# Keeping silu(g) and the rotary's swapped product in PSUM, and moving the first expert weights' splits ahead of the convolution's layer norm

## The chip, the cores and the metric

The kernel runs on one core of one Trainium2 chip. The metric is the device time of one execution in microseconds, as the median of several runs. The engines are TensorE (PE, with its weight loads as PEld), VectorE (DVE), ScalarE (ACT), GpSimd (POOL) and SyncE (SP), which here only issues DMA transfers.

## What is computed

Two layers over 256 tokens of width 1024. Each has a mixer and a feed-forward part, each followed by a residual layer norm. The mixer projects the input to six parts: a gated pair for a causal depthwise convolution of 31 taps, q and k (rotated), v, and a gate g. In the first layer the feed-forward part is a dense SwiGLU, in the second a mixture of 8 experts, two for each token. Everything is float32. Cut to what matters:

```python
glu_a, glu_b, q, k, v, g = split(x @ w_in)
u = silu(layer_norm(causal_conv(glu_a * sigmoid(glu_b)) + conv_b))
r = retention(rotary(q), rotary(k) / 8, v)          # 4 heads, chunks of 64
r = silu(g) * (group_norm(r) * ret_gn_g)
mix = concat([u, r]) @ w_out
x = layer_norm(ALPHA * x + mix)
# rotary: x1 * cos - x2 * sin, x1 * sin + x2 * cos
# layer 0: f = swiglu(x); layer 1: f = the two chosen experts' swiglu, weighted by their gates
x = layer_norm(ALPHA * x + f)
```

## The kernel before

**Split products.** A float32 product is made of three fast ones (`mm3`, lines 152 to 156): each operand is split into a high part and a rest, and high x high, high x rest and rest x high are summed. A split (`parts`, lines 107 to 110) is a cast on ScalarE (L109) and a subtraction on VectorE, or on GpSimd where `eng` is `gp` (both are L110). Weights come in units of 1 MB, 128 x 2048; each is loaded by one DMA into a buffer (`fetch`, L132) and split as two halves. `plan` fixes the order of all units and the engine of each half (lines 165 to 197); `W.take()` hands out the next half and `W.ahead(n)` splits up to n halves in advance. The order of instructions on each engine is the order of the program text, since the schedule is manual. All weight loads are issued by SyncE in that order, as soon as a buffer is free. Buffers are taken from a list (`seq`): seven `raw` buffers in the mixers; behind them the list is set anew to one `raw`, six `raw2` and four `raw`, then two of `once` and the one of `main`, and then repeats 13 buffers.

**Mixer** (`mixer`, lines 367 to 639). VectorE does the convolution one tap at a time (L387, L391), reading the input `u` from SBUF and its running sum from PSUM; `fill(n)` puts n of these steps between other work, and `fill(-1)` does the rest. The last 11 or 12 taps of the fourth channel block go to TensorE (`taps`, L407). Rotary (lines 437 to 446), per token tile: the swapped halves times sine into `t2` (L441, twice), the product with cosine into `qk` (L444), and their sum (L446). Then retention, its group norm (`gnorm`: statistics on VectorE, L489 on ScalarE, a multiply by `gn` on GpSimd, L492), the projection of g, the taps, and per token tile silu(g) into `sgt` (L584) and its product with `rz` (L585). TensorE transposes `rz` (L497), ScalarE copies it to `mr` (L498), and the retention half of the output product runs for three of four accumulators (L506). When the convolution is done, its transposes (L516), its layer norm (`conv_ln`, with the power L250 on GpSimd) and the convolution half of the output product follow. All PSUM tiles of this phase come from one pool of eight banks (`bank`).

**From mixer 1 to the experts.** The layer norm of token tile 0 is shared out over VectorE, ScalarE and GpSimd, that of tile 1 is on VectorE (L259 to L278). Then x is transposed (L291), copied (L292), multiplied with the router (`logits`, L320), and `choose` picks two experts per token (lines 303 to 316, tiny VectorE operations). x is split into high and rest as well (`parts`, tile 0 with GpSimd). Behind this the ranks `rk` are formed (L724 to L731), the selection `P` (L742), and `gather` collects the tokens of two experts by products with `P` (L751), whose results are split again (`gah`, `gal`, `gbh`, `gbl`). The experts' loop takes 56 blocks of six units each.

**What the change and the prediction touch.** `plan` for the experts (line 192); `rotary` (439); `sgt` (577, 584, 585); the places of `W.ahead(2)` and `W.ahead(4)` (628, 638); `parts` of x tile 0 (627) against `choose(0)` (629).

Of the kernel before, what the change touches and what calls it, by code (L numbers as in the profile page):

```python
# [11 lines left out]
F32 = mybir.dt.float32  # L12
# [3 lines left out]
AF = mybir.ActivationFunctionType  # L16
ALU = mybir.AluOpType
# [9 lines left out]
NT = S // 128  # L27
# [17 lines left out]
MOEP = {1: 0}  # L45
# [29 lines left out]
def tile_hybrid(ctx: ExitStack, tc, xT_in, x_in, ws, wm, cols, lnp, gnp, router, ident_in, rot, mask_in, out):  # L75
    nc = tc.nc
    v, sc, pe, gp = nc.vector, nc.scalar, nc.tensor, nc.gpsimd
# [13 lines left out]
    def f32(ap):  # L91
        return ap.bitcast(F32)
# [5 lines left out]
    def tok(t):  # L98
        return slice(128 * t, 128 * t + 128)

    def half(h):
        return slice(512 * h, 512 * h + 512)
# [4 lines left out]
    def parts(hi, lo, src, eng=None):  # L107

        sc.copy(hi, src)  # L109
        (eng or v).tensor_tensor(lo, src, f32(hi), op=ALU.subtract)  # L110
# [35 lines left out]
    W = Stream(emit)  # L146

    def plan(src, eng=None, kinds=("first", "second")):
        unit = src if isinstance(src, Unit) else Unit(src, eng)
        W.items += [(k, unit) for k in kinds]  # L150
# [14 lines left out]
    for l in range(DEPTH):  # L165
        b = l * MIXU
# [21 lines left out]
    for i, (e, b) in enumerate(blocks):  # L188
        prev_w2 = [wm[blocks[i - 1][0], 6 * blocks[i - 1][1] + q] for q in (4, 5)] if i else []
        for q in range(4):  # L190
            first = i == 0 and q < 2
            plan(Unit(wm[e, 6 * b + q], tuple(gp if first and q == 0 or MOEP.get(q) == h else None for h in range(2)),
                      at=0 if first and q else None))
        for w in prev_w2:
            plan(w)
# [21 lines left out]
    x = main.tile([128, NT, D], F32, tag="x", name="x")  # L217
# [68 lines left out]
    def turn_x(t, psum):  # L286

        for k in range(0, KD, 4):
            p = psum.tile([128, 4, 128], F32, tag="wk", name="wk")
            for j in range(4):  # L290
                pe.transpose(p[:, j, :], x[:, t, 128 * (k + j):128 * (k + j) + 128], ident)  # L291
            sc.copy(xf[:, k:k + 4, tok(t)], p)  # L292

    def part_x():
        for k in range(0, KD, 4):
            parts(xh[:, k:k + 4, :], xl[:, k:k + 4, :], xf[:, k:k + 4, :])

    xn = [w.rearrange("p (t k) s -> p t (k s)", t=NT) for w in X]
# [4 lines left out]
    def choose(t, lg):  # L303

        for n, (m, s) in enumerate(((m1, s1), (m2, s2))):
            v.tensor_reduce(m[:, t:t + 1], lg, axis=AX.X, op=ALU.max)
            q = sm.tile([128, NE], F32, tag="rq", name="rq")
            v.scalar_tensor_tensor(q, lg, m[:, t:t + 1], ie[:, t, :], op0=ALU.is_equal, op1=ALU.mult)
            i = sm.tile([128, 1], F32, tag="ri", name="ri")
            v.tensor_reduce(i, q, axis=AX.X, op=ALU.min)  # L310
            v.tensor_scalar(s[:, t, :], ie[:, t, :], i[:, 0:1], None, op0=ALU.is_equal)
            if n == 0:
                l2 = sm.tile([128, NE], F32, tag="rl", name="rl")
                v.scalar_tensor_tensor(l2, s1[:, t, :], -3.0e38, lg, op0=ALU.mult, op1=ALU.add)
                lg = l2
        v.tensor_tensor(sel[:, t, :], s1[:, t, :], s2[:, t, :], op=ALU.add)

    def logits(pl, t):
        for k in range(KD):
            pe.matmul(pl[:, t, :], xf[:, k, tok(t)], rt[:, k, :], start=k == 0, stop=k == KD - 1, skip_group_check=True)  # L320
# [8 lines left out]
    def bank(psum, shape):  # L329
        return psum.tile(shape, F32, tag="wk", name="wk")  # L330
# [36 lines left out]
    def mixer(l, psum, mp, me, heads, then):  # L367
# [8 lines left out]
        qkT = mp.tile([128, 2, 2, S], F32, tag="qkT", name="qkT")  # L376
        qk = mp.tile([128, NT, 512], F32, tag="qk", name="qk")
        PT = mp.tile([128, H, 384], F32, tag="PT", name="PT")
        rz = me.tile([128, NT, 512], F32, name="rz")
# [29 lines left out]
        def fill(n):  # L409

            while convs and n:
                g = convs.pop(0)
                if next(g, 0) is None:
                    convs.insert(1, g)
                    n -= 1
# [11 lines left out]
        def proj():  # L427

            ps = [bank(psum, [128, 512]) for t in range(NT)]
            for k in range(0, KD, 2):  # L430
                w = view(W.take(), "p (k f) -> p k f", k=2)
                for t, p in enumerate(ps):
                    for j in range(2):
                        mm3(p, two(X, A, k + j, tok(t)), two(w, A, j), k + j == 0, k + j == KD - 1)
            return ps

        def rotary(t, p):
            pv = p.rearrange("p (g s d) -> p g s d", g=8, s=2)
            t2 = me.tile([128, 8, 2, 32], F32, tag="t2", name="t2")
            for s in range(2):  # L440
                v.tensor_tensor(t2[:, :, s, :], pv[:, :, 1 - s, :],  # L441
                                rott[:, t, 1, 32 * s:32 * s + 32].unsqueeze(1).to_broadcast([128, 8, 32]), op=ALU.mult)
            o = qk[:, t, :].rearrange("p (g d) -> p g d", g=8)
            v.tensor_tensor(o, p.rearrange("p (g d) -> p g d", g=8),  # L444
                            rott[:, t, 0, :].unsqueeze(1).to_broadcast([128, 8, 64]), op=ALU.mult)
            v.tensor_tensor(qk[:, t, :], qk[:, t, :], t2.rearrange("p g s d -> p (g s d)"), op=ALU.add)  # L446
# [19 lines left out]
        def retain(t):  # L466
            p = bank(psum, [128, H, DV])
            for h in range(H):
                for j in range(t + 1):
                    c0 = 256 if j else 128 * t  # L470
                    pe.matmul(p[:, h, :], PT[:, h, c0:c0 + 128], vt[:, j, 128 * h:128 * h + 128],
                              start=(j == 0), stop=(j == t), skip_group_check=True)
            return p
# [20 lines left out]
        def turn_r(t):  # L494
            p = bank(psum, [128, 4, 128])
            for k in range(4):
                pe.transpose(p[:, k, :], rz[:, t, 128 * k:128 * k + 128], ident)  # L497
            sc.copy(mr[:, :, tok(t)], p)  # L498
# [4 lines left out]
        def wout_r(t, h):  # L503
            acc[t][h] = bank(psum, [128, 512])
            for k in range(4):
                pe.matmul(acc[t][h], mr[:, k, tok(t)], Wr[k // 2][:, k % 2, half(h)], start=k == 0, stop=False,  # L506
                          skip_group_check=True)
# [66 lines left out]
        fill(next(F))  # L574
        glu(3)
        fill(next(F))
        sgt = mp.tile([128, NT, 512], F32, tag="qkT", name="sgt")
        pr = [retain(t) for t in range(NT)]
        gnorm(pr)
        pg = proj()  # L580
        taps()
        fill(next(F))
        for t in range(NT):
            sc.activation(sgt[:, t, :], pg[t], AF.Silu)  # L584
            v.tensor_tensor(rz[:, t, :], rz[:, t, :], sgt[:, t, :], op=ALU.mult)  # L585
            fill(next(F))
        if l == 0:
            nc.sync.dma_start(x, x_in)
# [3 lines left out]
        for t in range(NT):  # L592
            turn_r(t)
        Wc += [W.take(0) for _ in range(4)]
        wout_r(0, 0)
        wout_r(0, 1)
        wout_r(1, 0)
# [26 lines left out]
                    heads = then(psum)  # L624
            ln_end(t, x, s, st, gt, ASIDE and l > 0 and t == 0)
        if l > 0:
            parts(xn[0][:, 0, :], xn[1][:, 0, :], x[:, 0, :], gp)
            W.ahead(2)
            choose(0, pl[:, 0, :])
        turn_x(NT - 1, psum)  # L630
        if l == 0:
            part_x()
            W.ahead(3)
        else:
            logits(pl, 1)
            parts(xn[0][:, 1, :], xn[1][:, 1, :], x[:, 1, :])
            choose(1, pl[:, 1, :])
            W.ahead(4)
        return heads


# [51 lines left out]
    with tc.tile_pool(name="ps1", bufs=8, space=bass.MemoryType.PSUM) as psum:  # L693
        busy(WARM, bank(psum, [128, 512]))
        with (tc.tile_pool(name="mp0", bufs=1, side="right", reuse_waits="tile") as mp,
              tc.tile_pool(name="me0", bufs=1, side="right", reuse_waits="tile") as me):
            heads = mixer(0, psum, mp, me, [], head)
        with tc.tile_pool(name="dp", bufs=1, side="right", reuse_waits="tile") as dp:
            heads = dense(psum, dp, heads)
        with (tc.tile_pool(name="mp1", bufs=1, side="right", reuse_waits="tile") as mp,  # L700
              tc.tile_pool(name="me1", bufs=1, side="right", reuse_waits="tile") as me):
            mixer(1, psum, mp, me, heads, None)
# [113 lines left out]
    def tokens_of(e0):  # L816
        pls = ((mo, "ga"), (mo, "gb") if e0 % 4 == 0 else (late[0], "gc"))
        g = gather(lambda i, t: rk[:, t, e0 + i:e0 + i + 1], 2, pls, mo if e0 % 4 == 0 else late[0])
        gs, PT = next(g)
        for i in range(2):  # L820
            got[e0 + i] = (gs[i], PT[:, i, :])
        return g
# [3 lines left out]
            pass  # L826

    g0 = tokens_of(0)
    cnt = mo.tile([128, 1], F32, name="cnt")
    v.tensor_reduce(cnt, pr[:, 2, :], axis=AX.X, op=ALU.max)  # L830
    cnti = mo.tile([128, 1], I32, name="cnti")
# [261 lines left out]
```

## Time and profile before

| | |
|---|---|
| median of 3 runs | 1488.01 us (1486.11 to 1498.08) |
| the profiled run | 1490.48 us, its span 1488.7 us |
| PE busy | 1438.5 us, 97% of the span |
| DVE busy | 1234.3 us, 83% |
| ACT busy | 973.8 us, 65% |
| POOL busy | 276.1 us, 19% |
| loads from HBM | 433.69 MB, 292 GB/s over the span |

Layer 0's mixer takes the first 120 us, the dense part the time to about 350, layer 1's mixer to about 454; the experts begin at 473.6 with the gather and run to about 1480. The table's shares are means over these stages, which have different limits. A timeline row has start, duration, engine, line, operation, output and inputs, shapes and the number of instructions that it merges; in brackets stands the engine's idle time before it and what ended that. A `q` behind an engine means its sequencer or queue.

### The profile page before, as it was taken

What the parts mean: (1) busy time and instruction counts of PE and PEld (TensorE: products, weight loads), DVE (VectorE), ACT (ScalarE), POOL (GpSimd) and SP (SyncE); (2) the same over time, 40 slices, a digit from 0 to 9 for tenths busy, and PEclk for the clock granted to TensorE, in tenths of its full rate; (3) what the DMA queues carried; (4) which work ended last, traced back from release to release, by engine and by line L of the source; (5) the groups of instructions that cost most, each with busy time, mean ns of one, the idle gap of its engine ahead of it and who ended that gap; (6) DMA issues with size and microseconds to landing.
All of it is one profiled execution on the core that took longest, in us unless ns stands there. A gap on an engine that the chain in (4) does not pass through costs nothing. (4 is left out here: it accounts for less than half of the span.)

```text
span 1488.7 us, 19729 instructions
## 1 busy us (share of the span) xinstructions
PE 1438.5 (97%) x7385; PEld 1208.2 (81%) x7385; DVE 1234.3 (83%) x1401; ACT 973.8 (65%) x1153; POOL 276.1 (19%) x138
## 2 busy tenths in 40 slices
PE   9989999999987999999999999999999999999995
PEld 8859999998856887778878877888887888888884
DVE  7976455547987899889899998999899899999896
ACT  6334344434443877768877767777877777787773
POOL 5630000002844113111111111111111111111111
PEclk9999999999997999999999999999999999999998
DMA  9535544545547888979999997999998899999951
GB/s 368 208 113 227 194 175 183 211 161 182 183 164 310 311 312 336 343 300 356 382 342 378 367 356 302 368 371 352 378 376 304 342 376 354 363 373 370 353 216 59
DMA packets 62311, 436.10 MB, mean 293 GB/s; under 512 B 7040, under 2 KB 7424, under 8 KB 9856
## 3 DMA queue, kind: packets, MB, share of 16 engines
q1 hardware_dynamic: 61920, 434.24, 77.4%
q8 instruction: 60, 0.98, 0.3%
q10 hardware_dynamic: 288, 0.52, 0.1%
q14 instruction: 43, 0.35, 0.1%
HBM read 433.69 MB, written 1.05 MB: 292 GB/s over the span
## 5 line engine op out<-in xcount | busy, mean ns | idle before, releaser
L110 DVE TENSOR_TENSOR wl<-raw,wh 128x1024 fp32r<-128x1024 f32 (+1 forms) x704 | 880.5, 1289 | 61.2 <-ACT wh L109 35.8
L109 ACT CAST wh<-raw 128x1024 fp32r<-128x1024 f32 (+1 forms) x802 | 820.8, 1045 | 160.2 <-PE ac L156 94.7
L110 POOL TENSOR_TENSOR wl<-raw,wh 128x1024 fp32r<-128x1024 f32 x98 | 241.9, 2484 | 1107.3 <-ACT wh L109 1062.5
L155 PE MATMUL ac<-wl,gah 128*128 128x512 f32 x448 | 175.2, 391 | 2.8 <-DVE wl L110 2.3
L154 PE MATMUL ac<-wh,gah 128*128 128x512 f32 x448 | 177.4, 396 | 0.0
L154 PE MATMUL y<-wh,hth 128*128 128x512 f32 x440 | 172.8, 393 | 3.6 <-DVE ys1l L110 3.6
L155 PE MATMUL y<-wl,hth 128*128 128x512 f32 x440 | 172.0, 391 | 3.8 <-DVE wl L110 3.8
L156 PE MATMUL ac<-wh,gal 128*128 128x512 f32 x448 | 175.1, 391 | 0.0
L156 PE MATMUL y<-wh,htl 128*128 128x512 f32 x448 | 174.5, 390 | 0.0
L154 PE MATMUL wk<-xh,wh 128*128 128x256 f32 x512 | 145.4, 284 | 1.8 <-ACT wh L109 1.8
L156 PE MATMUL wk<-xh,wl 128*128 128x256 f32 x512 | 145.0, 283 | 0.2 <-DVE wl L110 0.2
L155 PE MATMUL wk<-xl,wh 128*128 128x256 f32 x512 | 144.7, 283 | 0.0
L391 DVE SCALAR_TENSOR_TENSOR wk<-u,colt,wk 128x256 f32<-128x256 f32 x209 | 99.8, 489 | 5.7
L154 PEld LDWEIGHTS y<-wh,hth 128*128 128x128 f32 x440 | 82.6, 188 | 24.3 <-DVE ys1l L110 6.6
L155 PEld LDWEIGHTS ac<-wl,gah 128*128 128x128 f32 x448 | 84.4, 188 | 21.4 <-DVE wl L110 3.6
L155 PEld LDWEIGHTS y<-wl,hth 128*128 128x128 f32 x440 | 82.6, 188 | 22.4 <-DVE wl L110 5.6
L154 PEld LDWEIGHTS wk<-xh,wh 128*128 128x128 f32 x512 | 97.4, 190 | 3.4 <-ACT wh L109 2.2
L156 PEld LDWEIGHTS wk<-xh,wl 128*128 128x128 f32 x512 | 99.1, 194 | 0.7 <-DVE wl L110 0.7
L156 PEld LDWEIGHTS ac<-wh,gal 128*128 128x128 f32 x448 | 84.3, 188 | 17.8
L156 PEld LDWEIGHTS y<-wh,htl 128*128 128x128 f32 x448 | 84.1, 188 | 17.4
L155 PEld LDWEIGHTS wk<-xl,wh 128*128 128x128 f32 x512 | 97.5, 190 | 0.9
L154 PEld LDWEIGHTS ac<-wh,gah 128*128 128x128 f32 x448 | 84.4, 188 | 16.6
(202 smaller groups left out, 2055.1 us busy)
## 6 DMA issues: line engine op xcount, KB each, us to landing
raw<-in_wm_dram SPq DMA_DIRECT2D x336, 1024.0 KB, 7.0
raw<-in_ws_dram SPq DMA_DIRECT2D x68, 1024.0 KB, 5.0
raw<-in_lnp_dram SPq DMA_DIRECT2D x4, 1024.0 KB, 5.0
raw<-in_ws_dram SPq DMA_DIRECT2D x8, 256.0 KB, 5.5
xf<-in_xT_dram SPq DMA_DIRECT2D x4, 256.0 KB, 4.7
x<-in_x_dram SPq DMA_DIRECT2D x1, 1024.0 KB, 7.5
mask<-in_mask_dram SPq DMA_DIRECT2D x1, 768.0 KB, 12.7
gn<-in_gnp_dram SPq DMA_DIRECT2D x2, 256.0 KB, 8.3
```

The lines of the kernel that those rows point to most:

```text
L109: sc.copy(hi, src)
L110: (eng or v).tensor_tensor(lo, src, f32(hi), op=ALU.subtract)
L154: pe.matmul(o, a[0], b[0], start=first, stop=False, skip_group_check=True)
L155: pe.matmul(o, a[0], b[1], start=False, stop=False, skip_group_check=True)
L156: pe.matmul(o, a[1], b[0], start=False, stop=last, skip_group_check=True)
L391: v.scalar_tensor_tensor(d, u[:, cc, k:k + S], w[:, k:k + 1], o, op0=ALU.mult, op1=ALU.add)
```

## The change

- The rotary's swapped product `t2` becomes a PSUM tile from the pool of eight banks instead of an SBUF tile. L441 writes it and L446 reads it as before.
- silu(g) is written in place over `pg` in PSUM; the SBUF tile `sgt` goes, and the product with `rz` reads `pg`.
- The first two halves of the experts' weights (first unit, both with GpSimd as before) are split ahead of the first output products of mixer 1, instead of behind its last layer norm.
- x tile 0 is split with VectorE instead of GpSimd, behind `choose(0)` instead of ahead of it.
- The second unit's first half is split with VectorE instead of GpSimd, and both of its halves come behind the selection `P` of the first gather (`tokens_of(0)`), when the list of buffers has been set anew, instead of ahead of it.

```diff
@@ -189,7 +189,7 @@
         prev_w2 = [wm[blocks[i - 1][0], 6 * blocks[i - 1][1] + q] for q in (4, 5)] if i else []
         for q in range(4):
             first = i == 0 and q < 2
-            plan(Unit(wm[e, 6 * b + q], tuple(gp if first and q == 0 or MOEP.get(q) == h else None for h in range(2)),
+            plan(Unit(wm[e, 6 * b + q], tuple(gp if (q == 0 if first else MOEP.get(q) == h) else None for h in range(2)),
                       at=0 if first and q else None))
         for w in prev_w2:
             plan(w)
@@ -436,7 +436,7 @@
 
         def rotary(t, p):
             pv = p.rearrange("p (g s d) -> p g s d", g=8, s=2)
-            t2 = me.tile([128, 8, 2, 32], F32, tag="t2", name="t2")
+            t2 = bank(psum, [128, 8, 2, 32])
             for s in range(2):
                 v.tensor_tensor(t2[:, :, s, :], pv[:, :, 1 - s, :],
                                 rott[:, t, 1, 32 * s:32 * s + 32].unsqueeze(1).to_broadcast([128, 8, 32]), op=ALU.mult)
@@ -574,15 +574,14 @@
         fill(next(F))
         glu(3)
         fill(next(F))
-        sgt = mp.tile([128, NT, 512], F32, tag="qkT", name="sgt")
         pr = [retain(t) for t in range(NT)]
         gnorm(pr)
         pg = proj()
         taps()
         fill(next(F))
         for t in range(NT):
-            sc.activation(sgt[:, t, :], pg[t], AF.Silu)
-            v.tensor_tensor(rz[:, t, :], rz[:, t, :], sgt[:, t, :], op=ALU.mult)
+            sc.activation(pg[t], pg[t], AF.Silu)
+            v.tensor_tensor(rz[:, t, :], rz[:, t, :], pg[t], op=ALU.mult)
             fill(next(F))
         if l == 0:
             nc.sync.dma_start(x, x_in)
@@ -592,6 +591,8 @@
         for t in range(NT):
             turn_r(t)
         Wc += [W.take(0) for _ in range(4)]
+        if l > 0:
+            W.ahead(2)
         wout_r(0, 0)
         wout_r(0, 1)
         wout_r(1, 0)
@@ -624,9 +625,8 @@
                     heads = then(psum)
             ln_end(t, x, s, st, gt, ASIDE and l > 0 and t == 0)
         if l > 0:
-            parts(xn[0][:, 0, :], xn[1][:, 0, :], x[:, 0, :], gp)
-            W.ahead(2)
             choose(0, pl[:, 0, :])
+            parts(xn[0][:, 0, :], xn[1][:, 0, :], x[:, 0, :])
         turn_x(NT - 1, psum)
         if l == 0:
             part_x()
@@ -635,7 +635,6 @@
             logits(pl, 1)
             parts(xn[0][:, 1, :], xn[1][:, 1, :], x[:, 1, :])
             choose(1, pl[:, 1, :])
-            W.ahead(4)
         return heads
 
 
@@ -826,6 +825,7 @@
             pass
 
     g0 = tokens_of(0)
+    W.ahead(4)
     cnt = mo.tile([128, 1], F32, name="cnt")
     v.tensor_reduce(cnt, pr[:, 2, :], axis=AX.X, op=ALU.max)
     cnti = mo.tile([128, 1], I32, name="cnti")
```

## Rows read from the trace of the kernel before

**Rows 1.** The page's first line: the span.

```profile
span 1488.7 us, 19729 instructions
```

**Rows 2.** Busy us by stretch: PE, PEld, DVE, ACT, POOL, clock, DMA, GB/s.

```profile
15.00:76.10 61.10, 61.10 (x371) 53.86 (x370) 55.67 (x125) 31.54 (x53) 44.98 (x20) 1.00 0.71 279
...
76.10:80.80 4.70, 1.58 (x10) 1.35 (x10) 4.46 (x5) 1.14 (x3) 4.70 (x3) 0.83 0.13 16
...
421.76:426.40 4.64, 1.15 (x9) 0.91 (x9) 4.61 (x5) 0.59 (x1) 3.54 (x2) 1.00 0.58 201
...
454.00:473.60 19.60, 12.12 (x84) 10.70 (x83) 16.73 (x35) 7.91 (x10) 13.38 (x8) 0.60 0.83 319
...
600.00:1450.00 850.00, 840.06 (x3815) 689.45 (x3816) 773.95 (x703) 655.90 (x714) 118.11 (x48) 1.00 0.92 349
```

**Rows 3.** Timeline of PE, both mixers and the router.

```profile
43.26 0.39 PE L156 MATMUL wk<-wh,xl 128*128 128x512 f32 x1
...
43.49 1.04 PE L452 MATMUL wk<-ident,qk 128*128 128x128 f32 x8
...
77.12 0.65 PE L497 MATMUL wk<-ident,rz 128*128 128x128 f32 x4 [1.02 <-DVE rz L585]
...
79.87 1.11 PE L497 MATMUL wk<-ident,rz 128*128 128x128 f32 x4 [2.10 <-DVE rz L585]
...
80.78 11.37 PE L506 MATMUL wk<-raw,mr 128*128 128x512 f32 x24
...
426.40 10.47 PE L506 MATMUL wk<-raw,mr 128*128 128x512 f32 x24
...
465.94 3.55 PE L320 MATMUL wk<-rt,xf 128*128 128x8 f32 x16 [1.40 <-DVE rl L314]
```

**Rows 4.** VectorE by source line: calls, ns min/median/max, first and last start.

```profile
L446 DVE TENSOR_TENSOR qk<-qk,t x4: 691/1993/2848, 37.8 to 383.7; 128x512 f32<-128x512 f32 x4
...
L585 DVE TENSOR_TENSOR rz<-rz,sgt x4: 801/2629/2825, 76.3 to 423.4; 128x512 f32<-128x512 f32 x4
...
L444 DVE TENSOR_TENSOR qk<-wk,rott x4: 676/680/682, 37.1 to 383.0; 128x512 f32<-128x512 f32 x4
```

**Rows 5.** Timeline of ACT, both mixers.

```profile
75.53 1.13 ACT L584 ACTIVATE sgt<-wk 128x512 f32<-128x512 f32 x2
...
396.11 0.39 ACT L420 ACTIVATE sgl<-wk 128x256 f32<-128x256 f32 x1 [4.96 <-PE wk L156]
```

**Rows 6.** Timeline of DVE, rotary and end of the convolution.

```profile
42.36 1.14 DVE L446 TENSOR_TENSOR qk<-qk,t 128x512 f32<-128x512 f32 x1
...
91.47 0.48 DVE L391 SCALAR_TENSOR_TENSOR cv<-u,colt,wk 128x256 f32<-128x256 f32 x1
...
436.84 0.42 DVE L394 TENSOR_TENSOR cv<-cv,wk 128x256 f32<-128x256 f32 x1
```

**Rows 7.** Timeline of DVE, from the last layer norm to the gather.

```profile
457.10 0.75 DVE L278 SCALAR_TENSOR_TENSOR x<-s,rs,raw 128x512 f32<-128x512 f32 x1 [0.44 <-POOL rs L250]
...
457.77 2.84 DVE L272 SCALAR_TENSOR_TENSOR s<-s,mv,raw 128x512 f32<-128x512 f32 x1
...
460.65 2.71 DVE L278 SCALAR_TENSOR_TENSOR x<-s,rs,raw 128x512 f32<-128x512 f32 x1
...
463.93 1.66 DVE L311 TENSOR_SCALAR s<-ie,ri 128x8 f32<-128x8 f32 x1
...
471.65 1.22 DVE L110 TENSOR_TENSOR wl<-raw,wh 128x1024 fp32r<-128x1024 f32 x1
```

**Rows 8.** Timeline of POOL, layer 1.

```profile
438.86 0.54 POOL L250 TENSOR_TENSOR rs<-ve,neghalf 128x1 f32<-128x1 f32 x1 [8.31 <-DVE ve L248]
...
457.38 2.68 POOL L110 TENSOR_TENSOR xl<-x,xh 128x1024 fp32r<-128x1024 f32 x1 [0.32 <-ACT xh L109]
...
460.02 5.54 POOL L110 TENSOR_TENSOR wl<-raw,wh 128x1024 fp32r<-128x1024 f32 x2
```

**Rows 9.** Waits of the DMA queue: us in total, times, longest.

```profile
SPq L132 <- DVE wl L110: 991.0, 350, 13.4
```

## The prediction, made before the change was run

> **What bounds the kernel now.** I read the page first for the span: 1488.7 us [rows 1], in a run of 1490.48 us, 0.2% above the median of 1488.01. The sum below is made in the profiled span's own times; the saving is then taken off the median. Next the busy time by stretch: TensorE is busy for 61.10 of 61.10 us in the first part of layer 0's mixer, and for 840 of 850 us in the experts [rows 2]. There only TensorE work counts. What can be saved lies in three stretches: 76.1 to 80.8 (PE busy 1.58 of 4.70), 421.76 to 426.4 (1.15 of 4.64) and 454 to 473.6 (12.1 of 19.6, at a mean clock of 0.60, so part of it at 1.2 GHz) [rows 2]. Then the timelines of these stretches engine by engine, to see which wait ends last in each.
>
> In the first two, TensorE has done the taps and waits for `rz`: 1.02 us for token tile 0 and 2.10 us for tile 1 [rows 3], released by VectorE's multiply L585. That multiply has both inputs in SBUF. Its four calls took 0.80, twice about 2.63, and 2.83 us; the add L446, of the same kind and size, took 0.69 at best and 2.85 at worst [rows 4]. The long ones stand where GpSimd is running its 2.4 us splits (L110). A 128x512 operation with one input in PSUM (L444) took 0.68 us in all four calls [rows 4], beside the same splits. So VectorE waits for GpSimd where both of its inputs are in SBUF, and not where one is in PSUM. In the third stretch the same shows in the layer norm: two operations that take 0.75 us elsewhere take 2.84 and 2.71 [rows 7], while GpSimd splits `x` and the first expert unit [rows 8].
>
> **The change, part by part.** *Swapped product and silu(g) in PSUM.* L446 and L585 get one PSUM input, so I cost them at 0.69, by L444. Per call that removes: L446, 7.5 us in sum over four calls (0.69 + 2.85 + 2 x 1.99) less 4 x 0.69: 4.8 us; L585, 8.9 less 2.8: 6.1 us [rows 4]. What of it reaches the end goes by TensorE's order:
>
> Layer 0. Of the rotary's calls here one took 2.85 and the other 1.14 [rows 6], so VectorE is 2.6 us earlier behind them. It has no wait up to L585, and every input there is ready earlier. The silu, at 75.53 [rows 5], stands on ScalarE behind three casts, and these behind the group norm's scalings, which wait for VectorE's statistics; all of it comes 2.6 us earlier: 72.9, with both tiles done at 74.1. The multiplies then end near 75.0 instead of 79.8. TensorE's taps end at 76.1, now the last to come. Tile 0's transposes start at 76.1 instead of 77.12, tile 1's follow at once, and the output product L506 starts at about 77.4 (1.3 us behind the first transposes, for the ScalarE copy) instead of 80.78. It took 11.37 us here and 10.47 in layer 1 [rows 3], the difference being the low clock of 76.1 to 80.8 (0.83 in [rows 2]); without the waits I take 10.5. So it ends at 87.9 instead of 92.15: 4.2 us. Next late would be VectorE's convolution: it took 79.8 to 91.95 [rows 6], 12.1 us, and now ends at 87.1, just in time.
>
> Layer 1. Here the rotary's gain is lost again: VectorE came to the third gated unit at 396.7 and needs a sigmoid that ScalarE ends at 396.50, because TensorE is no earlier [rows 5]; 0.2 us stays. The L585 gain does the rest: multiplies at 420.1 and 421.2, done at 421.9 instead of 425.9. L506 starts at 423.1 (421.76 + 1.3) instead of 426.40, and ends 3.3 us earlier, at 433.6. The convolution ended at 437.26 [rows 6] and needs 11.4 us behind the multiplies: 433.3, again just in time. 3.3 us.
>
> What this adds: two PSUM tiles in each mixer, in a pool of eight banks, and `pg`'s banks are held to the multiply instead of the silu. The next user of those banks is the output product, behind the multiply anyway: nothing. ScalarE writing PSUM is not in the trace. Its nearest rows are 0.57 us each for the silu [rows 5]; if a call were free or took double, 0.6 us either way, the 1.0 us by which tile 0 is early in layer 1 covers it. L441 now writes PSUM; its price lies between its present 0.41 and the 0.49 of a convolution step, which writes PSUM at the same width: at most 0.6 us for all eight, under cover.
>
> The row is 0.68 for the PSUM operand against 0.69. [...]
>
> *First expert unit's splits ahead of the layer norm, x parts off GpSimd, second unit's first half off GpSimd.* The DMA queue keeps its order: no other load stands between the old and the new place, and the queue runs ahead of the other engines (it waits for freed buffers, 991 us in sum) [rows 9]. The second unit now takes its buffer from the ring that follows, so all later units move up one place; the ring has 13 buffers, 13 units of lead, and one fewer still leaves twelve: nothing. The two casts go to ScalarE behind the last output weight, where it is idle until the convolution ends. On GpSimd the splits come between the last output weight's split and the layer norm's power (L250), where it was idle for 8.31 us; the two took 5.54 where they stood, with VectorE in their way [rows 8]. That leaves 2.8 us. Without this cover the power, and the whole norm behind it, would be late by up to 2.8 us a split.
>
> Now the path behind the norm, in the old clock. L272 and L278 for the second halves, 2.84 and 2.71 us, become about 0.7 each, as the first half's 0.75 [rows 7], so x is whole at 459.2 instead of 463.36: 4.15 us. `choose(0)` follows at once; its L311 falls from 1.66 to 0.23 [rows 7], so its last read of the logits' bank, for which the router product waited (1.40 us [rows 3]), is over at 460.3; it ends at 461.4. Then VectorE splits x tile 0 (1.22, new here), to 462.6, and tile 1, to 463.8. Meanwhile TensorE transposes at 459.26, ScalarE copies to 461.0, and the router product L320 runs for 3.55 us at the low clock [rows 3], 461.05 to 464.6 instead of 465.94 to 469.49: 4.9 us. It ends behind the two splits by 0.8 us, so they are hidden; without that cover they cost 1.22 each. `choose(1)` ends at 466.8. Behind it the old order had a weight split of 1.22 us on VectorE at 471.65 ahead of `rk` [rows 7]; now `rk` goes first: 0.7 us. The gather starts 5.6 us earlier. Its own parts now stand behind two weight splits on VectorE (2.4 us, by the same row); in front of the first product that needs them TensorE has 16 gather products and two others, over 4 us at the low clock. Nothing. 5.6 us.
>
> Sum: 4.2 + 3.3 + 5.6 = 13.1 us; dense layer and experts pass it on, since TensorE bounds both. 1488.0 - 13.1 = **1475 us**.
>
> **Rivals.** *Clock stays up or comes back sooner.* The low clock covers the router and gather. If the shorter gaps keep it at 2.4 GHz, the router product takes half of its 3.55 us, but VectorE's two x splits then bind (0.8 of the 1.8 is left), and the gather's products, some 2 us shorter, wait about 1 us for those two weight splits. About 2 us: 1473, and 1471 with a luckier start. Against: the transposes and router products stay as thin as they are.
>
> *Part is lost.* If ScalarE or the convolution turns out late where I have 0.2 to 1 us of cover, the 4.2 falls to about 2.5 and the 3.3 to 2.5; if GpSimd's power waits for the early splits, up to 5.5 us more comes on the path: 1478 to 1483.
>
> *Banks.* With the swapped products, all eight banks are spoken for at the rotary: two by the convolution, two by the first gated products, two by the q and k projection, two by the new tiles. If the second projection were given a bank that the rotary still holds, TensorE would stop until the last add. It starts at about 32.6 in layer 0 (43.49 less 48 products of 0.227) [rows 3] and that add would end near 40.9: 8.3 us (the last add's 42.36 [rows 6], less 2.2, plus 0.69). If layer 1 lost as much, and a low clock stood behind both stops (0.9 each, as found above), that is 18.4 us more: 1493, slower than before by 5 us. It decides from 13.1 us of such waits. For: no bank is spare. Against: the first products' banks are free before that in both layers, since VectorE has read them.
>
> *It doesn't do what it says.* If PSUM inputs waited for GpSimd too, the first 7.5 us would go and 1482 would be left. Against: L444 and the convolution steps (0.49) run beside the same splits.
>
> **How the numbers follow.** Forecast 0.60 (its own range 1472.5 to 1478); clock up 0.13; part lost 0.20; banks 0.04; no effect of PSUM 0.03. Leaving out the ends beyond 1470.5 and 1481 leaves out under 2 in 10: range 1470.5 to 1481. One per cent is 14.9 us, which is about what a measurement can tell from no change, and the forecast lies just inside it: faster takes the clock case and a sixth of the forecast's, 0.23; slower by over 1% needs more than one mishap, 0.02; same 0.75.
>
> **What would show it.** L446 and L585 at 0.7 us in all calls, and no wait of TensorE for `rz` behind the taps; L506 about 4 and 3 us earlier. L272 and L278 at 0.75 throughout behind the last norm, GpSimd with nothing but the power there; gather start near 460.5 in the new span (473.6 less 13.1). Wrong if TensorE waits at the second projection, if the power is held by splits, or if the experts take longer than before.

## The result and the profile after

The changed kernel took 1474.7 us (median; 1473.94 to 1476.35), the kernel before, on the same chip, 1487.53 us: ratio 0.991, 95% interval 0.988 to 0.993. A second measurement on another chip gave 1475.28 against 1487.9 us, ratio 0.992 (0.990 to 0.993). Forecast were 1475.0 us, in a range of 1470.5 to 1481.

The page's first line answers [rows 1]:

```profile
span 1472.2 us, 19728 instructions
```

VectorE by source line, of the kernel after (calls, ns min/median/max, first and last start). L584 was L585, a line above it having gone:

```profile
L446 DVE TENSOR_TENSOR qk<-qk,wk x4: 686/689/689, 35.7 to 375.9; 128x512 f32<-128x512 f32 x4
...
L584 DVE TENSOR_TENSOR rz<-rz,wk x4: 678/680/686, 71.6 to 415.0; 128x512 f32<-128x512 f32 x4
...
L441 DVE TENSOR_TENSOR wk<-wk,rott x8: 423/430/432, 34.1 to 374.9; 128x256 f32<-128x256 f32 x8
```

Where [rows 4] had up to 2.85 us, no call of L446 or L584 is now over 0.69.

Timeline of PE, both mixers and the router, as in [rows 3]:

```profile
74.48 1.04 PE L497 MATMUL wk<-ident,rz 128*128 128x128 f32 x8
75.76 10.57 PE L506 MATMUL wk<-raw,mr 128*128 128x512 f32 x24 [0.24 <-ACT mr L498]
...
415.56 1.04 PE L497 MATMUL wk<-ident,rz 128*128 128x128 f32 x8
416.83 10.57 PE L506 MATMUL wk<-raw,mr 128*128 128x512 f32 x24 [0.24 <-ACT mr L498]
...
451.01 3.56 PE L320 MATMUL wk<-rt,xf 128*128 128x8 f32 x16
```

TensorE no longer waits for `rz`: the transposes L497 run as eight in a row in both layers, and 0.24 us for ScalarE's copy is the whole gap ahead of L506. The router product L320 still takes 3.56 us, against 1.90 us for the same product of tile 0: the granted clock is 0.50 over the one (451.01 to 454.57) and 1.00 over the other (446.00 to 448.00). The traces give the clock as a share of the full one and no frequency; where the prediction and the expectations write 2.4 and 1.2 GHz, the traces have 1.00 and 0.50.

Timeline of DVE behind the last layer norm, as in [rows 7]:

```profile
447.66 0.75 DVE L278 SCALAR_TENSOR_TENSOR x<-s,rs,raw 128x512 f32<-128x512 f32 x1 [0.44 <-POOL rs L250]
448.33 0.74 DVE L272 SCALAR_TENSOR_TENSOR s<-s,mv,raw 128x512 f32<-128x512 f32 x1
449.11 0.75 DVE L278 SCALAR_TENSOR_TENSOR x<-s,rs,raw 128x512 f32<-128x512 f32 x1
...
450.43 0.23 DVE L311 TENSOR_SCALAR s<-ie,ri 128x8 f32<-128x8 f32 x1
...
451.90 2.35 DVE L110 TENSOR_TENSOR xl<-x,xh 128x1024 fp32r<-128x1024 f32 x2
454.60 0.17 DVE L306 TENSOR_REDUCE m<-wk 128x1 f32<-128x8 f32 x1 [0.35 <-PE wk L320]
```

L272, L278 and L311 have fallen from 2.84, 2.71 and 1.66 us to 0.74, 0.75 and 0.23. The two x splits are over 0.35 us before VectorE can go on with the router product: they are hidden.

Timeline of POOL around the moved splits, answering [rows 8]:

```profile
411.63 13.95 POOL L110 TENSOR_TENSOR wl<-raw,wh 128x1024 fp32r<-128x1024 f32 x6
429.38 0.54 POOL L250 TENSOR_TENSOR rs<-ve,neghalf 128x1 f32<-128x1 f32 x1 [3.81 <-DVE ve L248]
```

The splits end in time for the norm's power with 3.81 us to spare.

Busy us by stretch (PE, PEld, DVE, ACT, POOL, clock, DMA, GB/s), answering [rows 2]:

```profile
75.76:86.33 10.57, 10.57 (x26) 4.78 (x27) 8.68 (x19) 1.38 (x2) 3.10 (x2) 1.00 0.51 195
444.00:458.30 14.30, 12.23 (x87) 10.80 (x86) 11.66 (x36) 6.12 (x8) 2.70 (x5) 0.71 0.89 357
600.00:1435.00 835.00, 825.11 (x3752) 677.27 (x3751) 760.05 (x692) 643.68 (x702) 116.02 (x48) 1.00 0.92 348
```

The experts are as before: TensorE is busy for 825 of 835 us, and for 840 of 850 in [rows 2].

**Where the time went.** Both kernels and all experiments, cut at rows of their timelines: the start of ScalarE's first copy of `vt` (L564) in each mixer, the start of the last L278 of each mixer's own layer norm, and the first product `ac` of the experts. The column to `vt` of layer 1 thus holds the dense part. All in us:

| kernel | to `vt`, layer 0 | to last L278, layer 0 | to `vt`, layer 1 | to last L278, layer 1 | to first `ac` | rest |
|---|---|---|---|---|---|---|
| before, as predicted from | 42.32 | 72.44 | 273.45 | 72.44 | 16.52 | 1011.5 |
| before, profiled again | 41.69 | 70.17 | 273.45 | 74.12 | 15.73 | 1010.4 |
| after | 40.86 | 68.06 | 273.44 | 66.75 | 12.56 | 1010.5 |
| after, profiled again | 41.60 | 68.34 | 273.47 | 66.93 | 12.58 | 1010.7 |
| PSUM alone | 42.08 | 68.33 | 273.46 | 68.82 | 15.10 | 1010.5 |
| splits alone | 41.88 | 69.46 | 273.46 | 71.71 | 12.55 | 1010.8 |
| silu alone | 41.24 | 68.14 | 273.46 | 69.02 | 15.73 | 1010.8 |
| rotary alone | 40.95 | 69.18 | 273.48 | 74.96 | 15.05 | 1010.6 |
| rotary, wait filled | 44.04 | 68.48 | 273.45 | 72.09 | 15.06 | 1010.9 |
| x part back on GpSimd | 42.58 | 68.14 | 273.46 | 69.02 | 12.57 | 1010.4 |
| splits at the old place | 41.88 | 68.08 | 273.47 | 68.84 | 14.50 | 1010.4 |
| splits behind the norm | 42.41 | 68.48 | 273.48 | 68.75 | 12.54 | 1010.5 |
| clock kept, 1st / 2nd | 42.31 / 42.55 | 68.35 / 68.07 | 273.46 / 273.45 | 66.93 / 66.73 | 11.54 / 12.80 | 1010.8 / 1010.7 |

The column with the dense part is the same to 0.04 us in all of them. The first profiles of the two kernels differ by 16.5 us of span, more than the medians do (12.8): 1.46 us of it lies ahead of the first `vt`, which starts anywhere from 40.86 to 44.04 us in the fourteen profiles, without regard to the change (at 44.04 in a run whose granted clock was 0.50 from 22.79 to 26.20), and 1.0 us in the rest. The profiled run of before was also 2.5 us above its median. The second profiles differ by 12.0 us.

### The profile page after: what moved, and what is told of

It reads as the page before. It is cut to its first block, busy times and chain, and to the rows that moved or that the text cites. A ratio compares the mean times of both kernels' runs of the same rounds, so it can differ in the third digit from the quotient of the medians.

```text
span 1472.2 us, 19728 instructions
## 1 busy us (share of the span) xinstructions
PE 1433.5 (97%) x7385; PEld 1204.0 (82%) x7385; DVE 1220.2 (83%) x1403; ACT 973.4 (66%) x1153; POOL 266.4 (18%) x136
## 5 line engine op out<-in xcount | busy, mean ns | idle before, releaser
L110 POOL TENSOR_TENSOR wl<-raw,wh 128x1024 fp32r<-128x1024 f32 x97 | 234.7, 2435 | 1107.1 <-ACT wh L109 1047.9
L154 PEld LDWEIGHTS y<-wh,hth 128*128 128x128 f32 x440 | 82.6, 188 | 24.2 <-DVE ys1l L110 6.6
L155 PEld LDWEIGHTS y<-wl,hth 128*128 128x128 f32 x440 | 82.6, 188 | 22.3 <-DVE wl L110 5.6
```

The costliest lines, as they stand in the source:

```text
L154: pe.matmul(o, a[0], b[0], start=first, stop=False, skip_group_check=True)
L155: pe.matmul(o, a[0], b[1], start=False, stop=False, skip_group_check=True)
```

## The experiments

**The two halves of the change.** First the PSUM edits alone, in the kernel before:

```diff
-        t2 = me.tile([128, 8, 2, 32], F32, tag="t2", name="t2")
+        t2 = bank(psum, [128, 8, 2, 32])
...
-            sc.activation(sgt[:, t, :], pg[t], AF.Silu)
-            v.tensor_tensor(rz[:, t, :], rz[:, t, :], sgt[:, t, :], op=ALU.mult)
+            sc.activation(pg[t], pg[t], AF.Silu)
+            v.tensor_tensor(rz[:, t, :], rz[:, t, :], pg[t], op=ALU.mult)
```

> The kernel before with the two PSUM edits alone (silu in place, the swapped product in a bank). My theory, that VectorE's long multiplies were long only because both inputs lay in SBUF while GpSimd split weights: every L446 and every product of the gate at 0.68 to 0.69 us, tap sums 4.4 us earlier in layer 0 (net of the start) and 3.4 us earlier in layer 1, the gather as late after the last layer norm as in the kernel before, whole gain 7.5 us (ratio 0.995). Rival, that what the changed kernel won in the mixers came from the splits being issued at another place (another phase against VectorE): below 3 us, with multiplies of over 2 us still there. The two halves are additive: this gain and that of the splits alone sum to the 13 us of the whole change; if they overlap, both are larger than their shares.

Then the opposite: the changed kernel with these lines taken back.

> The changed kernel with the swapped product and silu(g) back in SBUF tiles, so that only the moved splits and the x parts on VectorE are left. My theory: L446 and the product again reach 2 to 2.85 us, the mixers are as long as before; from the last layer norm to the first product of the experts 5.6 us shorter, whole gain 5 to 6.5 us (ratio 0.996). Rival, that the early splits only move the collision: four more splits of GpSimd lie beside VectorE's work around the conv's layer norm and make it 1 to 3 us later there, whole gain 3 to 4.5 us.

PSUM alone: 1480.09 against 1487.19 us, ratio 0.9951 (0.9933 to 0.9968), 7.3 us. Splits alone: 1482.0 us, 0.9965 (0.9943 to 0.9987), 5.2 us. Together 12.5 us, against 12.4 and 14.0 us by the ratios of the whole change: within their intervals, of some 2.5 to 3.3 us either way, the halves add up. VectorE by source line, first with PSUM alone, then with the splits alone:

```profile
L446 DVE TENSOR_TENSOR qk<-qk,wk x4: 687/689/691, 36.6 to 377.4; 128x512 f32<-128x512 f32 x4
...
L584 DVE TENSOR_TENSOR rz<-rz,wk x4: 678/680/687, 72.5 to 416.5; 128x512 f32<-128x512 f32 x4
```

```profile
L446 DVE TENSOR_TENSOR qk<-qk,t x4: 691/950/2846, 36.8 to 380.3; 128x512 f32<-128x512 f32 x4
...
L585 DVE TENSOR_TENSOR rz<-rz,sgt x4: 810/2634/2834, 73.1 to 420.0; 128x512 f32<-128x512 f32 x4
```

So it is the operand's place that takes the long cases away, not the phase of the splits, and the first rival falls. The second, that the early splits make the convolution's layer norm 1 to 3 us later, can't be told by time, since the interval of 5.2 us reaches from 1.9 to 8.5. The traces speak against it: from the eight products L506 behind the convolution to the first L278 of tile 1 it is 19.57 us with the splits alone and 19.51 before. One point did not fit: in layer 0, splits alone needed 69.46 us, only 1.1 more than with PSUM, where the prediction has 4.2.

**Silu alone and rotary alone**, each half of the diff above in the kernel before.

> The kernel before with silu(g) in place in PSUM alone. My theory: 3.3 us in layer 0 and 3.2 us in layer 1, 6.5 us in all (ratio 0.9956), products at 0.68 us, L446 still with its long cases. Rival, that TensorE's taps wait for something else (the turned retention mr from ScalarE, the conv's tap sums) and take up the gain: 2 to 4 us.

> The kernel before with the swapped product in PSUM alone. My theory: 0.9 us in layer 0, none in layer 1 (VectorE waits there for ScalarE's sgl behind the rotary), 1 us in all, within what can be measured (ratio 0.998 to 1.000); L446 at 0.69 us, the product of the gate still up to 2.8 us. If the later collisions shift, the products collide more or less than before: 2 us either way. Rival, that the rotary's gain is kept in both layers: 2.5 to 3.5 us.

Silu: 1480.63 us, ratio 0.9949 (0.9931 to 0.9967), 7.6 us. Rotary: 1486.74 us, 0.9988 (0.9969 to 1.0007), not to be told from nothing. The silu carries the whole: with it alone the rotary's sums still take up to 2.86 us, and layer 0 is as short (68.14 us) as with both edits (68.33). But the rotary's profile has a layer 1 of 74.96 us, longer than before's 72.44. Its PE timeline there:

```profile
418.15 0.66 PE L497 MATMUL wk<-ident,rz 128*128 128x128 f32 x4 [1.19 <-DVE rz L585]
420.91 1.11 PE L497 MATMUL wk<-ident,rz 128*128 128x128 f32 x4 [2.10 <-DVE rz L585]
421.81 12.95 PE L506 MATMUL wk<-raw,mr 128*128 128x512 f32 x24
```

L506 took 12.95 us, where [rows 3] have 10.47 in the same layer: the granted clock was 0.81 over it, and 0.81 over the 4.85 us ahead of it; with a clock of either 1.00 or 0.50 that is 6.8 us at 0.50. TensorE had just stood idle for 1.19 and 2.10 us.

**Is the profile of before the rule?** Two more kernels. The kernel before again, unchanged:

> The kernel before, profiled once more. My theory: which of the rotary's sums and gate's products fall on a split of GpSimd changes with the start of the run by tenths of a microsecond (two of four L446 and three of four products in the first profile, but one L446 in the run with the splits alone), each that does costs 2.1 us on VectorE, and where TensorE then stands idle for it its clock may fall to 1.2 GHz for the next 3.4 to 6.8 us. So the number of long ones, or the layer in which the clock falls, differs from the first profile, at the same total within 1.5 us. Rival: the same multiplies are long and the clock falls in layer 0 again, so that the first profile's row is the rule.

It gave 1488.03 us, ratio 1.0005 (0.998 to 1.003). Its PE timeline in both layers:

```profile
77.32 0.66 PE L497 MATMUL wk<-ident,rz 128*128 128x128 f32 x4 [1.00 <-DVE rz L585]
77.81 10.46 PE L506 MATMUL wk<-raw,mr 128*128 128x512 f32 x24
...
423.01 1.12 PE L497 MATMUL wk<-ident,rz 128*128 128x128 f32 x4 [2.10 <-DVE rz L585]
423.92 11.72 PE L506 MATMUL wk<-raw,mr 128*128 128x512 f32 x24
```

Now layer 0 has one wait of 1.00 us and a fast L506, and layer 1 the slow one: the reverse of [rows 3]. The rotary's first sum took 1.95 us, not 2.85. The split of GpSimd that it met (POOL) and the sum (DVE) in their timelines, in the first profile of before and then in this one:

```profile
37.67 2.46 POOL L110 TENSOR_TENSOR wl<-raw,wh 128x1024 fp32r<-128x1024 f32 x1
37.82 2.85 DVE L446 TENSOR_TENSOR qk<-qk,t 128x512 f32<-128x512 f32 x1
```

```profile
35.11 2.45 POOL L110 TENSOR_TENSOR wl<-raw,wh 128x1024 fp32r<-128x1024 f32 x1
36.16 1.95 DVE L446 TENSOR_TENSOR qk<-qk,t 128x512 f32<-128x512 f32 x1
```

Both sums end about 0.55 us behind the split that was running when they started: 40.67 against 40.13 us, and 38.11 against 37.56. So do all 60 calls of L446, L585, L272 and L278 that took over 0.78 us in the fourteen profiles (0.54 to 0.55 us). What such a call costs depends on what is left of the split when it starts: from nothing up to 2.2 us more than 0.69, which moves with tenths of a microsecond of phase.

The two mixers together took 144.29 us against 144.88 of the first profile. So the loss is there in both, but where it falls is a matter of chance. (Expected was a total within 1.5 us: the medians are, the spans of the two profiles differ by 3.1, most of it outside the mixers.)

Second, the rotary kernel with TensorE's waits in layer 1 filled by products that nobody reads:

```diff
+        bk = bank(psum, [128, 512]) if l > 0 else None
         for t in range(NT):
+            if l > 0:
+                busy((18, 32)[t], bk)
             turn_r(t)
```

> The kernel before with the swapped product in PSUM (silu(g) still in SBUF) and, in layer 1 alone, 18 and 32 matmuls on ones in the two waits of TensorE for the gate's products. My theory: the waits stay (1.2 and 2.1 us), but the clock no longer falls in them, so that the 24 products of the retention (L506) take 10.5 us in place of 12.95 us: 2 to 2.5 us less than the kernel with the rotary alone, about 1484 us; what silu(g) in PSUM still brings over it is 4 to 5 us. Rival, that the clock's fall has another cause than the idle time: L506 still 11.4 to 13 us, no gain.

Its PE timeline in layer 1, and behind it the busy us of the window over L506 (columns as above):

```profile
419.16 1.17 PE L326 MATMUL wk<-ones 128*128 128x128 bf16 x18
420.52 0.66 PE L497 MATMUL wk<-ident,rz 128*128 128x128 f32 x4 [0.19 <-DVE rz L585]
421.01 1.95 PE L326 MATMUL wk<-ones 128*128 128x128 bf16 x32
423.29 0.66 PE L497 MATMUL wk<-ident,rz 128*128 128x128 f32 x4 [0.32 <-DVE rz L585]
423.78 10.46 PE L506 MATMUL wk<-raw,mr 128*128 128x512 f32 x24
```

```profile
423.78:434.25 10.47, 10.47 (x28) 4.68 (x27) 9.70 (x21) 1.53 (x2) 2.35 (x1) 1.00 0.28 115
```

The clock stays at 1.00, L506 takes 10.46 us, and layer 1 falls from 74.96 to 72.09 us. The whole: 1484.83 against 1487.9 us, ratio 0.9973 (0.9957 to 0.9989), where rotary alone had 0.9988; by the ratios 2.2 us apart, with intervals that overlap. That the idle time caused the fall is therefore made likely, not shown: without filling, a wait of 2.10 us came five times in four profiles (both layers in the first profile of before, layer 1 in the second, in splits alone and in rotary alone), and one of them, layer 1 of [rows 3], brought no fall either. Silu alone is still 3.6 us ahead of the filled kernel by the ratios (0.9949), with intervals that overlap a little.

**The splits' place and the x part.** Three kernels made from the changed one: x's first tile part back on GpSimd ahead of `choose(0)`; the first unit's two splits back behind the last norm; and these two splits just behind the convolution's norm. No run takes back the second unit's move alone.

```diff
+            parts(xn[0][:, 0, :], xn[1][:, 0, :], x[:, 0, :], gp)
             choose(0, pl[:, 0, :])
-            parts(xn[0][:, 0, :], xn[1][:, 0, :], x[:, 0, :])
```

> The changed kernel with the subtraction of x's first token tile back on GpSimd, ahead of the first choice of experts. My theory: it starts when that tile's norm is done, beside the norm of the second tile, so that one L272 or L278 takes 2.7 to 2.85 us in place of 0.74: the second tile, the router and the gather 2 us later than in the changed kernel, less 1.2 us of subtraction that leaves VectorE: 1 to 2 us slower than the changed kernel, 11 to 12 us faster than before. Rival, that the norm's operations were long before only because of the splits queued behind the x part: nothing lost, up to 1 us won.

```diff
-        if l > 0:
-            W.ahead(2)
         wout_r(0, 0)
...
         if l > 0:
+            W.ahead(2)
             choose(0, pl[:, 0, :])
```

> The changed kernel with the two units' splits back behind the last layer norm, x parts still on VectorE. My theory: the splits of 5.5 us for a pair run beside L272, L278 and the choice of experts, two to three of which take 1.7 to 2.85 us: the gather 3.5 to 5 us later than in the changed kernel, 8 to 9.5 us faster than before; mixers as in the changed kernel. Rival, that x's part on GpSimd and not the splits was what VectorE collided with: within 1 us of the changed kernel.

```diff
-        if l > 0:
-            W.ahead(2)
         wout_r(0, 0)
...
         conv_ln(pc)
+        if l > 0:
+            W.ahead(2)
```

> The changed kernel with the two units' splits a little later in the program, behind the conv's layer norm and not ahead of it. Theory: the subtractions that make ml (0.42 us each, both inputs in SBUF) then run beside GpSimd's splits and take 1.7 us or more, two to four of them, ScalarE's casts of the weights (2 us) stand ahead of the copies of the turned conv, and the norms' power on GpSimd waits behind the splits: 4 to 7 us slower than the changed kernel, so the place ahead of the norm is needed. Rival, that any place ahead of the last norm does: at most 2 us slower.

Against 1488.23 us of before: 1477.58 (0.9922, 0.9897 to 0.9946), 1478.87 (0.9934, 0.991 to 0.9959) and 1478.11 us (0.9933, 0.9907 to 0.9959). All three intervals overlap that of the changed kernel (0.9881 to 0.9932), so what each step is worth is read from the traces. By the table, over the two columns from the `vt` of layer 1 to the first `ac` and against the first profile of after, they lose 2.3, 4.0 and 2.0 us. DVE and POOL in the first of them:

```profile
450.33 2.83 DVE L272 SCALAR_TENSOR_TENSOR s<-s,mv,raw 128x512 f32<-128x512 f32 x1
453.20 0.75 DVE L278 SCALAR_TENSOR_TENSOR x<-s,rs,raw 128x512 f32<-128x512 f32 x1
...
449.94 2.67 POOL L110 TENSOR_TENSOR xl<-x,xh 128x1024 fp32r<-128x1024 f32 x1 [0.32 <-ACT xh L109]
```

and in the second:

```profile
449.39 2.84 DVE L272 SCALAR_TENSOR_TENSOR s<-s,mv,raw 128x512 f32<-128x512 f32 x1
452.27 2.71 DVE L278 SCALAR_TENSOR_TENSOR x<-s,rs,raw 128x512 f32<-128x512 f32 x1
...
449.00 5.43 POOL L110 TENSOR_TENSOR wl<-raw,wh 128x1024 fp32r<-128x1024 f32 x2 [0.32 <-ACT wh L109]
```

One split of GpSimd makes one VectorE operation with two SBUF inputs 2.1 us longer, two make two. By these profiles both parts of the move were needed, and the 1.2 us that the x part takes off VectorE in the first brings nothing, since the choice of experts then waits for the router product instead. In the third, PE, ACT and DVE:

```profile
437.35 0.50 PE L154 MATMUL wk<-wh,mh 128*128 128x512 f32 x1 [2.37 <-ACT mh L109]
...
434.18 1.98 ACT L109 CAST wh<-raw 128x1024 fp32r<-128x1024 f32 x2
...
438.48 2.72 DVE L110 TENSOR_TENSOR ml<-sl,mh 128x256 fp32r<-128x256 f32 x3 [0.57 <-ACT mh L109]
```

The loss is ScalarE's two casts: TensorE waits 2.37 us for `mh`, after 0.70 in the changed kernel. The subtractions for `ml` did meet the splits (2.72 us for three, 0.42 each elsewhere), but TensorE had products to do. Expected were 4 to 7 us: too much, as the collisions were counted on the path. The rival's bound of 2 us came out; the place ahead of the norm is better, but by 2.0 us only in these profiles.

**Keeping the clock up in the router.** The changed kernel with 8 products on ones ahead of tile 1's first transposes and 14 ahead of its second, and the count `cnt` ahead of the fourth split:

```diff
         for k in range(0, KD, 4):
+            if bk is not None:
+                busy(8 if k == 0 else 14, bk)
...
-    W.ahead(4)
     cnt = mo.tile([128, 1], F32, name="cnt")
     v.tensor_reduce(cnt, pr[:, 2, :], axis=AX.X, op=ALU.max)
+    W.ahead(4)
```

> The changed kernel with 22 matmuls of 128 columns on ones put into TensorE's idle time between the first and the second tile's logits, and the count of the experts' tokens taken ahead of the next split. My theory: TensorE stays at 2.4 GHz from the router through the gather; the second logits take 1.9 us in place of 3.56 us, of which VectorE's x parts leave 0.35 us, the gather's products 0.11 us apart in place of 0.21 us, of which the split of wl (2.35 us) ahead of the gathered tokens' split leaves 0.3 to 0.9 us: 0.6 to 1.4 us faster than the changed kernel. Rival, that the added matmuls stand in the way of the second tile's transposes: no gain or up to 1 us slower. Either way within 1% of the changed kernel.

> The changed kernel itself, beside the runs below: 12.5 to 13.5 us faster than before (ratio 0.991). Its profile once more: if it is my theory that holds, no multiply of VectorE's rotary and gate is over 0.70 us and TensorE's clock is at 2.4 GHz from the start of the program's first products to the last layer norm of layer 1, as in its first profile; if that first profile was a lucky draw, a low stretch or a wait of 2.1 us is there again.

> The changed kernel with the matmuls on ones between the logits and the count ahead of the split, a second time, now beside the changed kernel itself. In its profile it was 1.0 us shorter from the last layer norm's end to the first product of the experts. My theory: 0.5 to 1.5 us faster than the changed kernel on the same chip. Rival: what is won there is lost at the start of the run, where the clock's rise moves by more than that from run to run: within 0.5 us.

First run: 1475.21 us, ratio 0.9908 (0.9881 to 0.9936). As expected, the router product kept the full clock (1.92 us for 3.56), and the stretch to the first `ac` was 1.0 us shorter than in the changed kernel. Not as expected, the clock fell as it ended, at 454.81 us: the first gather products took 0.41 us each, the last 0.28, at a granted clock of 0.66 from 453 to 463 us. Beside the changed kernel on one chip there was nothing left of it: 1475.69 us (0.9918, 0.9904 to 0.9932) against 1475.28. Two rows of windows, the first from the first run and the second from the second:

```profile
448.00:453.00 5.00, 4.55 (x50) 4.01 (x48) 4.28 (x13) 2.56 (x4) 1.12 (x3) 1.00 0.94 393
```

```profile
448.00:453.00 5.00, 5.00 (x46) 4.80 (x45) 4.28 (x13) 2.12 (x3) 1.11 (x3) 0.72 0.98 410
```

The second time the clock fell at 450.17 us, in a stretch in which TensorE is busy for 5.00 of 5.00 us, and for all of the 2.17 us ahead of the fall. The router product, at 453.42, took 1.94 us all the same, but all 16 gather products had the low clock (0.41 us each behind the first; granted 0.67 from 453 to 463 us), and that run's stretch to `ac` was 12.80 us. The filling does not hold the clock here every time, and no version beat the changed kernel. What decides when the clock falls stays open. The second profile of the changed kernel again has no L446 or L584 over 0.69 us, and a granted clock of 1.00 from 15 to 445 us.

## Why the prediction came out

**The long multiplies**: right. Of the rotary's sums and the gate's products, the run with PSUM alone has none over 0.70 us, the run with splits alone has them up to 2.85 and 2.83 again. For the same add that is 2.85 us with two SBUF inputs beside a split and 0.69 with one of them in PSUM. Two SBUF tensors are not the only case here: L311, with one tensor of 128x8 and a scalar for each token, took 1.66 us beside a split and 0.23 without; why is not shown.

**The price of the PSUM operand**: right to go by L444. L446 went from 0.691 at best to a median of 0.689 us, so no price of reading PSUM is seen. L441, now writing PSUM, takes 0.430 where the second profile of before has 0.415: 0.12 us for all eight, where up to 0.6 was allowed. The silu in place takes 1.11 us for the pair against 1.13 [rows 5].

**Layer 0, 4.2 us**: 4.4 between the profiles compared (72.44 less 68.06), by the steps written: with 1.46 us added for the earlier start, L506 begins at 77.2 in before's time (predicted 77.4). But that profile was an expensive draw. With the second profile of each it is 1.8 us (70.17 less 68.34). The term was mis-sized because one profile was read as the rule. The first rotary sum was taken at 2.85 us, but it took 1.95 the second time and 0.76 in the run with splits alone; VectorE came to the rotary 5.88 us ahead of the first `vt` in the first profile and 6.91 in the second; and the low clock behind the waits, 0.9 us of L506, was put into layer 0. In the second profile the sum of this left TensorE a single wait of 1.00 us for `rz`, with another of 0.73 us for VectorE's convolution behind L506. That also is the point which did not fit in the run with splits alone: it has 0.63 us for `rz` and the same 0.73 us.

**Layer 1, 3.3 us**: measured 5.7 and 7.2 by the table for layer 1 with the norm, of which 2.1 are the first of the two long norm operations, counted under the transition in the prediction. That leaves 3.6 and 5.1. The multiplies' share was right against the first profile, the rotary's gain was lost as forecast (VectorE waits 1.40 us for `sgl` behind it), and the 1.5 us between the two pairs goes with the clock fall (L506 took 11.72 us in the second profile of before), which the prediction has in layer 0 alone. Summed over both layers it had 7.5; the two pairs gave 8.0 and 6.9, the run with PSUM alone 7.3. Against the second pair, layer 0 was 2.4 us too high and layer 1 1.8 too low, and that these nearly cancel in the sum is in part luck: nothing in the prediction ties one to the other.

**From the last norm to the experts, 5.6 us**: 2.1 and 4.0 in the first pair (6.1), 2.1 and 3.2 in the second (5.2), and 5.2 by the run with splits alone (1.9 to 8.5). The router product came 14.93 us earlier, 5.5 more than what went before accounts for (predicted 4.9). The x splits were hidden as said, the router product ending 0.35 us behind them where 0.8 was forecast. GpSimd had 3.81 us left instead of 2.8. One wait was overlooked, of TensorE for `cnt`, behind the two weight splits: 0.30 us in the first profile of after, 1.09 in the second.

**Rivals.** *Banks*: no wait of TensorE at the second projection. *Part is lost*: the convolution was not late, TensorE's transposes of it (L516) start behind L506 without a wait in both layers. *Clock*: the router product took 3.56 us at a granted 0.50, so the clock did not stay up. A sooner return shows between the two profiles of before, whose stretches to `ac` differ by 0.8 us. In the second profile of after the gather had the full clock from its second product on (0.28 us, where the first profile has 0.41 at a granted 0.50 from 458 to 460), but TensorE then waited 1.09 us for `cnt`, about what the rival had for the weight splits, and the stretch was no shorter (12.58 against 12.56). *No effect of PSUM* fell with the first experiment.

## What to carry to other kernels

A VectorE operation that shares a stretch with GpSimd is worth giving one PSUM operand, where it is on the path and a bank is free until it is done: here each operation that met a split lost up to 2.2 us, and the PSUM operand cost 0.015 us per L441 and nothing that can be seen elsewhere. Off the path it brings nothing: the rotary's half alone gave a ratio of 0.9988 (0.9969 to 1.0007). Where that can't be done, move GpSimd's work to a stretch where VectorE's operations are off the path, and see what ScalarE has to issue with it, since that can cost as much (2.0 us by the table in the run with the splits behind the convolution's norm). One L278 of 2.84 us is left in the changed kernel, at 349.19 us, beside a split, and costs nothing: TensorE is in a run of 64 products (L345) there.

When a saving is read from a stall, look at the clock behind the stall too, and profile the kernel before twice: one pair of profiles gave layer 0 a gain of 4.4 us, the next 1.8, while the sum over both layers moved by 1.1 only.

## What was not expected of the hardware

TensorE's granted clock fell to 0.50 at the wait of 2.1 us in layer 0 in one profile of the kernel before (from 79.2 to 82.6 us), where the same wait in layer 1 brought no fall (1.00 from 421.76 to 436.87), and at that of layer 1 in the next (0.89 over L506); L506 then took 11.4 to 12.95 us in place of 10.5. Filled with idle products, the wait brought no fall (10.46 us) in the one profile taken. But in the router the clock fell in a second run of a kernel that had held it up to the router product in the first, with TensorE busy for 5.00 of 5.00 us, so that filling alone is not shown to be enough.

The wait of VectorE for GpSimd is sharper than a slowdown: an operation of 0.69 to 0.75 us with both inputs in SBUF that starts during a split ends 0.55 us behind it, in all 60 long calls, whether the split had 0.25 or 2.3 us left.
